# Sums of squares split into two tasks around a chunk of the z projection, with their low part made by VectorE

## The chip, the cores and the metric

The kernel runs on one core of a Trainium2 chip. The metric is the device time of one execution in microseconds (us), lower is better. Five engines work side by side, each through its own queue in a fixed order: TensorE (PE; its weight loads are shown apart as PEld), VectorE (DVE), ScalarE (ACT), GpSimd (POOL) and SyncE (SP), which here issues nearly all DMAs.

## The reference, cut to what matters

A hybrid decoder block on x of 1 x 1024 x 1024 in float32. After an RMS norm, one large projection gives the inputs of two attention branches and of their gates:

```
h = rms_norm(x, g_pre);  proj = h @ w_in
qa, ka, va, fa, za, qb, kb, vb, zb, gates = split(proj)
ya = fox_attention(qa, ka, va, log_sigmoid(fa + b)) * silu(za)      # 8 heads of 64
yb = diff_attention(rope(qb), rope(kb), vb, lam)                    # 4 heads, values of 128
yb = rms_norm(yb, g_subln, 1e-5) * (1 - lam_init) * silu(zb)        # norm over a head's 128 channels
merged = sigmoid(gates_a) * (ya @ w_branch[0]) + sigmoid(gates_b) * (yb @ w_branch[1])
out = x + rms_norm(merged @ w_out, g_post)
```

The change is in the norm inside `yb`: for each of the four diff heads and each of the 1024 positions it needs the sum of 128 squares.

## The kernel before, in words

Float32 products are made from a high and a low part (tiles `hi` and `lo`, or `hT[0]` and `hT[1]`): hi is a rounded copy, lo the difference, and three matmuls stand for one. `project` makes one 128 x 512 chunk of a projection in 24 such matmuls of 512 columns. Its weights come through `load_w`: a DMA into `raw`, hi by GpSimd (line 321), lo by VectorE (line 324).

The work runs in stages: the value projection; eight attention units (u = 0 to 3 diff heads, 4 to 7 pairs of forgetting heads); the gates; the branch products; the output projection. Inside a unit the attention itself is a list of `groups`, each of two score rows (`row`, `s_row`: matmuls into `S`, a VectorE pass with the running minimum, line 495, and an exponential on ScalarE, line 501) and of products (`av`: transposes on TensorE, line 522, hi by ScalarE, line 525, lo by VectorE, line 526, and matmuls into `yp`, line 546). Between the groups stand the `fill` tasks: the four chunks k, q, k, q of the next unit's projection (`unit_proj`), two chunks of one z tile (`z_tasks`, `spill_tasks`: 24 matmuls into `pz`, a copy to SBUF on line 433, a store), and in units 3 to 6 (`SFILL`) the sums of squares of one diff head: `sum_squares` for each half c of the positions and then `subln_scales`.

`sum_squares` loads half of the head's stored output `y_d` (line 442), squares it on ScalarE (443), makes hi on ScalarE (445) and lo on GpSimd (446), adds the 128 channels up by two matmuls with a matrix of ones (`onesr`, lines 448 and 449, into `ssq`), copies the one row out (450) and stores it (451). What it makes is read only after the attention, by `y_work`.

Three rings of buffers bind these steps. `pj` has two PSUM buffers, taken in turn by every k, q and z chunk and by `ssq`. The tag `sw` has two SBUF buffers: hi and lo of the squares take both, and the hi part of a k or q chunk (`stack`, lines 378 and 379, or `rope` for a diff unit) takes one. The tag `raw` has four.

Program order is a priority: a planner puts each engine's instructions into one fixed order by a simulated timeline, and takes what is ready in it, earlier program text first. `tc.issue_after(x)` adds that what is written in its block comes behind x in the order of x's engine. `lasts[0]` holds the last matmul that the program has written so far. How the fill tasks are dealt out is one line in the loop over the groups, where `done` counts the weight (4g + 3) of the groups so far:

```
while nf < len(fill) and nf < len(fill) * done * (3 if u == 7 else 1) / total:
    fill[nf]()
    nf += 1
```

Of the kernel before, what the change touches and what calls it, by code (L numbers as in the profile page):

```python
# [12 lines left out]
ALU = mybir.AluOpType  # L13
# [8 lines left out]
CH = 512  # L22
# [14 lines left out]
ZFILL = ((0,), (1,), (), (2,), (3,), (4,), (5,), (6, 7))  # L37
# [13 lines left out]
def tile_hybrid_block(  # L51
# [18 lines left out]
    nc = tc.nc  # L70
# [28 lines left out]
    onesr = const.tile([P, 32], F32R, name="onesr")  # L99
# [17 lines left out]
    def rstd_of(dst, ss, n, eps):  # L117
        nc.gpsimd.tensor_scalar(dst, ss, 1.0 / n, eps, op0=ALU.mult, op1=ALU.add)
        nc.gpsimd.tensor_tensor(dst, dst, mhalf[:, 0:dst.shape[-1]], op=ALU.pow)
# [220 lines left out]
    with ExitStack() as st:  # L340
# [75 lines left out]
        def z_tasks(t):  # L416
            return spill_tasks(f"z{t}", (ZA + t * P) if t < 4 else (ZB + (t - 4) * P), z_d[t])

        def spill_tasks(nm, c0, dst):
            box = {}  # L420

            def mk(c):
                def run(ks=range(KT)):
                    if not box:
                        box[0] = load_w(nm, w_cols(c0))
                    if ks[0] == 0:
                        box["ps"] = pj.tile([P, CH], F32, tag="pj", name=f"p{nm}_{c}")
                    ps = box["ps"]
                    lasts[0] = project(ps, box[0], c, ks)
                    if ks[-1] < KT - 1:  # L430
                        return
                    zs = stg.tile([P, CH], F32, tag="raw", name=f"s{nm}_{c}", bufs=4)
                    nc.scalar.copy(zs, ps)
                    nc.sync.dma_start(dst[:, c * CH:(c + 1) * CH], zs)
                return run
            return [mk(0), mk(1)]

        def sum_squares(t, c):

            sl = slice(c * CH, (c + 1) * CH)  # L440
            sq = stg.tile([P, CH], F32, tag="raw", name=f"sq{t}_{c}", bufs=4)
            nc.sync.dma_start(sq, y_d[t][:, sl])
            nc.scalar.activation(sq, sq, AF.Square)
            hi, lo = (stg.tile([P, CH], F32R, tag="sw", name=f"sq{part}{t}_{c}") for part in range(2))
            nc.scalar.copy(hi, sq)
            nc.gpsimd.tensor_tensor(lo, sq, hi, op=ALU.subtract)
            ps = pj.tile([P, CH], F32, tag="pj", name=f"ssq{t}_{c}")[0:32]
            nc.tensor.matmul(ps, lhsT=onesr, rhs=hi, start=True, stop=False)
            nc.tensor.matmul(ps, lhsT=onesr, rhs=lo, start=False, stop=True)
            nc.scalar.copy(sq[0:1], ps[0:1])  # L450
            nc.sync.dma_start(ss_d[t:t + 1, sl], sq[0:1])

        def subln_scales(t):
            rs = sub_rs[:, t]
            nc.sync.dma_start(rs, ss_d[t].rearrange("(p j) -> p j", j=8))
            rstd_of(rs, rs, P, SUB_EPS)
            nc.sync.dma_start(rs_d[t].rearrange("(p j) -> p j", j=8), rs)
# [21 lines left out]
        lastx, vload, lasts = [None], [], [None]  # L479
# [74 lines left out]
        def products(trans, prod, g):  # L554
            for jj in range(g + 1 + SKEW):
                if jj <= g:
                    trans(jj)
                if jj >= SKEW:
                    prod(jj - SKEW)
# [91 lines left out]
        def forget_sums():  # L651

            fgf = fg.rearrange("p a b -> p (a b)")
            fs = pp.tile([P, 4, 64], F32, tag="P", name="fs")
            fn, fe, fu, fc = (fs[:, n, :] for n in range(4))
            nc.vector.tensor_scalar(fn, fgf, -1.0, None, op0=ALU.mult)
            nc.vector.tensor_tensor(fn, fn, fgf, op=ALU.min)
            nc.scalar.activation(fe, fn, AF.Exp)
            nc.vector.tensor_scalar(fu, fe, 1.0, None, op0=ALU.add)
            nc.vector.tensor_scalar(fc, fu, -1.0, None, op0=ALU.add)  # L660
            nc.vector.tensor_tensor(fc, fe, fc, op=ALU.subtract)
            nc.scalar.activation(fn, fu, AF.Ln)
            nc.vector.reciprocal(fu, fu)
            nc.vector.tensor_tensor(fc, fc, fu, op=ALU.mult)
            nc.vector.tensor_tensor(fn, fn, fc, op=ALU.add)
            nc.vector.tensor_scalar(fe, fgf, 0.0, None, op0=ALU.min)
            nc.vector.tensor_tensor(fe, fe, fn, op=ALU.subtract)
            lf = pp.tile([8, S], F32, tag="P", name="lf")
            cum = pp.tile([8, S], F32, tag="P", name="cum")
            ones8 = pp.tile([8, S], F32, tag="P", name="ones8")  # L670
            nc.gpsimd.memset(ones8, 1.0)
            for half in range(2):
                tp = tps.tile([P, CH], F32, tag="tp", name=f"ft{half}")
                for q in range(4):
                        b = half * 4 + q
                        nc.tensor.transpose(tp[0:8, q * P:(q + 1) * P], fe[:, b * 8:(b + 1) * 8], ident)
                nc.scalar.copy(lf[:, half * CH:(half + 1) * CH], tp[0:8, :])
            nc.vector.tensor_tensor_scan(cum, ones8, lf, initial=0.0, op0=ALU.mult, op1=ALU.add)
            nc.vector.tensor_scalar(cum, cum, -8.0, None, op0=ALU.mult)
            nc.sync.dma_start(cum_d, cum)  # L680
# [7 lines left out]
        for u in range(8):  # L688
            load, load_v, groups = nxt or unit_attn(u, T)
            nxt = None  # L690
            if u == 0:
                vload.append(load_v)
            if u == 1:
                forget_sums()
            load()
            fill = []
            if u + 1 < 8:
                T, tasks = unit_proj(u + 1)
                fill += tasks
            for t in ZFILL[u]:  # L700
                fill += z_tasks(t)
            for t in SFILL[u]:
                fill += [lambda t=t, c=c: sum_squares(t, c) for c in range(2)]
                fill.append(lambda t=t: subln_scales(t))
            late = [fill.pop(), gate[0]] if u == 7 else []
            total = sum(s[0] for s in groups)
            done, nf = 0, 0
            for n, (wgt, rws, prd) in enumerate(groups):
                if n == len(groups) // 2 and u < 7:
                    nxt = unit_attn(u + 1, T)  # L710
                    vload.append(nxt[1])
                for r in rws:
                    r()
                mark = lasts[0]
                if pend and (u < 7 or n <= TAIL):
                    products(*pend())
                if u == 7 and n >= TAIL:
                    tail.append(prd)
                pend = prd
                done += wgt  # L720
# [3 lines that stand above are left out]
                if u == 7:  # L724
                    for f, a, b in LATE[n]:
                        with tc.issue_after(mark):
                            late[f](range(a, b))
                    if n == GFILL:
                        behind = tuple(held)
                        break  # L730
# [69 lines left out]
    sums = [None]  # L800
# [377 lines left out]
```

## Time and profile before

| what | value |
|---|---|
| median of 3 runs | 900.61 us (899.82 to 900.72) |
| the profiled execution's own time | 901.03 us |
| its span | 899.3 us, so 1.7 us lie around it |
| PE, PEld, DVE, ACT, POOL busy | 98%, 83%, 65%, 48%, 45% of the span |
| granted TensorE clock | 0.998 |

Busy times are shares of the span of one execution. PE counts the matmuls with modelled ends, PEld the weight loads. In an answer by stretches of time, the first number is the length of the stretch and the others are the busy time of each engine in it. In an answer in order of time, a row has its start, its length, its engine and line, what it writes and reads, and in brackets how long the engine was idle before it and what ended that. "PEld ssq L448 <- ACT sq L445: 1.1, 2, 0.8" says that weight loads of `ssq` on line 448 waited twice for ScalarE's line 445, 1.1 us in all and 0.8 us at most.

### The profile page before, as it was taken

How to read it: one execution, taken by the hardware profiler on the slowest of the kernel's cores; microseconds unless marked ns; L12 is line 12 of the kernel's file. 1: busy time of each engine (PE TensorE's matmuls, PEld its weight loads, DVE VectorE, ACT ScalarE, POOL GpSimd, SP SyncE). 2: the span in 40 equal slices, each digit the busy share in tenths (PEclk: the TensorE clock that was granted, in tenths of full speed). 3: DMA queues.
4: the chain of work that ended last, by engine and by line, in shares of the span. 5: the costliest groups of instructions: out<-in, count | busy, mean ns of one | idle time of the engine just before them, and what ended most of it. 6: DMA issues, size and time to landing. Idle time of an engine off the chain costs nothing.

```text
span 899.3 us, 13795 instructions
## 1 busy us (share of the span) xinstructions
PE 882.4 (98%) x4600; PEld 745.4 (83%) x4600; DVE 581.8 (65%) x1122; ACT 430.4 (48%) x865; POOL 406.0 (45%) x398
## 2 busy tenths in 40 slices
PE   8999999999999999999999999999999999999996
PEld 5999987788888878888888888888888888888885
DVE  6766555767666744456647556627766896648896
ACT  7523224665756653364545646724543362314352
POOL 2134224735646535254344435516534323483961
PEclk9999999999999999999999999999999999999999
DMA  8566656756557763645636430397766598210495
GB/s 303 191 241 249 221 160 166 176 139 170 154 136 188 183 172 80 184 98 133 188 94 158 137 105 26 85 410 243 240 200 203 185 359 299 80 39 1 124 194 173
DMA packets 138185, 154.79 MB, mean 172 GB/s; under 512 B 12145, under 2 KB 98161, under 8 KB 137090
## 3 DMA queue, kind: packets, MB, share of 16 engines
q1 hardware_dynamic: 133744, 151.55, 56.2%
q0 software_dynamic: 4224, 2.10, 2.0%
q8 instruction: 36, 0.59, 0.3%
q14 instruction: 35, 0.29, 0.1%
q10 hardware_dynamic: 146, 0.27, 0.1%
HBM read 86.17 MB, written 38.34 MB: 138 GB/s over the span
## 4 chain that ended last, share of the span: by engine, by line
PE 84%; DMA 4%; DVE 3%; ACT 3%; SPq 2%; issue 2%; POOL 2%; POOLq 0%; DVEq 0%; ACTq 0%
PE x_g L818 15%; PE pb L978 10%; PE pv L214 10%; PE pz L334 9%; PE x_o L818 9%; PE pk L334 7%; PE pq L334 6%; PE ypf L546 4%; PE ptf L522 3%; PE ypd L546 2%; PE Sf L492 2%; PE Sf L493 2%; PE pg L334 1%; SPq L366 1%; PE pgl L334 1%
## 5 line engine op out<-in xcount | busy, mean ns | idle before, releaser
L214 PE MATMUL pv<-wvhi,hT 128*128 128x264 f32 (+2 forms) x384 | 88.1, 323 | 1.0 <-ACT wvhi L160 1.0
L334 PE MATMUL pq<-hT,hi_q 128*128 128x512 f32 x256 | 82.1, 395 | 0.0
L334 PE MATMUL pz<-hT,hi_z 128*128 128x512 f32 x256 | 81.7, 394 | 0.3 <-DVE rotq L368 0.2
L334 PE MATMUL pk<-hT,hi_k 128*128 128x512 f32 x256 | 81.7, 393 | 0.0
L978 PE MATMUL pb<-yT,hi_br 128*128 128x512 f32 x256 | 78.8, 389 | 0.0
L818 PE MATMUL x_g<-T,a_g 128*128 128x512 f32 x336 | 78.0, 391 | 0.0
L818 PE MATMUL x_o<-wo_op,a_o 128*128 128x512 f32 x336 | 77.6, 392 | 0.0
L818 PEld LDWEIGHTS x_o<-wo_op,a_o 128*128 128x128 f32 x336 | 63.0, 188 | 14.4 <-DVE a_o L768 0.5
L818 PEld LDWEIGHTS x_g<-T,a_g 128*128 128x128 f32 x336 | 63.1, 188 | 13.8
L214 PEld LDWEIGHTS pv<-wvhi,hT 128*128 128x128 f32 x384 | 64.1, 190 | 7.2 <-ACT wvhi L160 1.7
L526 DVE TENSOR_TENSOR plf<-ptf,phf 128x512 fp32r<-128x512 f32 (+1 forms) x80 | 50.1, 635 | 25.8 <-ACT phf L525 25.1
L501 ACT ACTIVATE Pd<-Pd,mxd 128x128 f32<-128x128 f32 (+7 forms) x64 | 49.8, 778 | 33.6 <-DVE mxd L495 33.5
L618 POOL TENSOR_TENSOR cb<-cb,trim 128x128 f32<-128x128 f32 x64 | 29.3, 462 | 72.0 <-DVE mxf L495 49.9
L214 PE MATMUL pv<-wvlo,hT 128*128 128x256 f32 (+2 forms) x192 | 61.7, 326 | 0.0
L501 ACT ACTIVATE Pf<-Pf,mxf 128x1024 f32<-128x1024 f32 (+3 forms) x64 | 49.7, 777 | 24.4 <-DVE mxf L495 24.1
L818 PE MATMUL x_g<-hT,a_g 128*128 128x512 f32 x252 | 59.1, 392 | 0.0
L623 POOL TENSOR_SCALAR Pf<-Pf,lf 128x1024 f32<-128x1024 f32 (+3 forms) x64 | 47.9, 753 | 21.9 <-DVE lf L622 18.3
L525 ACT CAST phf<-ptf 128x512 fp32r<-128x512 f32 (+1 forms) x80 | 42.6, 543 | 30.7 <-PE ptf L522 26.5
L978 PEld LDWEIGHTS pb<-yT,hi_br 128*128 128x128 f32 x256 | 48.0, 188 | 10.1
L818 PEld LDWEIGHTS x_g<-hT,a_g 128*128 128x128 f32 x252 | 47.3, 188 | 10.4
L334 PEld LDWEIGHTS pz<-hT,hi_z 128*128 128x128 f32 x256 | 47.3, 188 | 9.4 <-DVE rotq L368 0.5
L334 PEld LDWEIGHTS pq<-hT,hi_q 128*128 128x128 f32 x256 | 47.2, 188 | 8.9
(262 smaller groups left out, 2282.1 us busy)
## 6 DMA issues: line engine op xcount, KB each, us to landing
t_d<-t SPq DMA_DIRECT2D x16, 512.0 KB, 4.1
T<-t_d SPq DMA_DIRECT2D x8, 1024.0 KB, 8.3
raw<-in_w_in_dram SPq DMA_DIRECT2D x14, 512.0 KB, 4.8
vb_d<-vbs SPq DMA_DIRECT2D x8, 512.0 KB
va_d<-vas SPq DMA_DIRECT2D x8, 512.0 KB, 3.3
raw_k<-in_w_in_dram SPq DMA_DIRECT2D x8, 512.0 KB, 4.5
raw_q<-in_w_in_dram SPq DMA_DIRECT2D x8, 512.0 KB, 4.7
V<-vb_d SPq DMA_DIRECT2D x4, 1024.0 KB, 6.3
```

Of the source, the lines that this page charges most:

```text
L214: nc.tensor.matmul(ps[n], lhsT=hT[hp][k // 4][i // 4][:, k % 4, hs], rhs=wt[k][:, a:b], start=first, stop=(k == KT - 1 and hp == 1))
L334: mm = nc.tensor.matmul(ps, lhsT=a[:, k, :], rhs=hT[h][k // 4][c][:, k % 4, :], start=(k == 0 and a is hi and h == 0), stop=(k == KT - 1 a ...
L492: nc.tensor.matmul(ps, lhsT=A[:, qs], rhs=B[:, a:b], start=True, stop=False)
L501: held[0] = nc.scalar.activation(pr[:, 0:n], pr[:, 0:n], AF.Exp, bias=mx[:, len(pcs) - 1:len(pcs)], scale=-1.0, accum_out=le).ins
L522: lasts[0] = nc.tensor.transpose(pt[:, o * P:(o + 1) * P], rows[2 * g + r][:, j * P:(j + 1) * P], ident).ins
L525: nc.scalar.copy(ph[:, 0:n], pt[:, 0:n])
L526: nc.vector.tensor_tensor(pl[:, 0:n], pt[:, 0:n], ph[:, 0:n], op=ALU.subtract)
L546: lasts[0] = nc.tensor.matmul(o, lhsT=a, rhs=b[:, src], start=(j == 0 and n == 0), stop=(odd == 1 and jj == g and n == len(prods) - 1)).ins
L618: nc.gpsimd.tensor_tensor(diag, diag, trim, op=ALU.add)
L623: held[1] = nc.gpsimd.tensor_scalar(p1[:, 0:n], p1[:, 0:n], l1, 1.0, op0=ALU.mult, op1=ALU.mult).ins
L818: nc.tensor.matmul(x[m], lhsT=a[:, ai, k, :], rhs=right[m][bi][k], start=(k == 0 and n == 0), stop=(k == 3 and n == 2))
L978: nc.tensor.matmul(ps, lhsT=a[:, kk, :], rhs=yT[g][h][:, k % 2, sl], start=(k == 0 and a is hi and h == 0), stop=(k == 3 and a is lo))
```

## The change

`sum_squares` becomes two tasks. `squares` loads, squares and makes hi and lo; `square_sums` does the two matmuls, the copy and the store. In the list of fill tasks of units 3 to 6 the order was z0, z1, both sums of squares, scales; now it is squares 0, z0, sums 0, squares 1, z1, sums 1, scales. The first matmul of the sums is ordered behind the last matmul written so far, which is the last one of the z chunk. The low part of the squares is made by VectorE in place of GpSimd.

```diff
         def sum_squares(t, c):
 
+            box = {}
+            return lambda: squares(t, c, box), lambda: square_sums(t, c, box)
+
+        def squares(t, c, box):
+
             sl = slice(c * CH, (c + 1) * CH)
             sq = stg.tile([P, CH], F32, tag="raw", name=f"sq{t}_{c}", bufs=4)
             nc.sync.dma_start(sq, y_d[t][:, sl])
             nc.scalar.activation(sq, sq, AF.Square)
             hi, lo = (stg.tile([P, CH], F32R, tag="sw", name=f"sq{part}{t}_{c}") for part in range(2))
             nc.scalar.copy(hi, sq)
-            nc.gpsimd.tensor_tensor(lo, sq, hi, op=ALU.subtract)
+            nc.vector.tensor_tensor(lo, sq, hi, op=ALU.subtract)
+            box.update(sq=sq, hi=hi, lo=lo)
+
+        def square_sums(t, c, box):
+
+            sl = slice(c * CH, (c + 1) * CH)
+            sq, hi, lo = box["sq"], box["hi"], box["lo"]
             ps = pj.tile([P, CH], F32, tag="pj", name=f"ssq{t}_{c}")[0:32]
-            nc.tensor.matmul(ps, lhsT=onesr, rhs=hi, start=True, stop=False)
+            with tc.issue_after(lasts[0]):
+                nc.tensor.matmul(ps, lhsT=onesr, rhs=hi, start=True, stop=False)
             nc.tensor.matmul(ps, lhsT=onesr, rhs=lo, start=False, stop=True)
             nc.scalar.copy(sq[0:1], ps[0:1])
             nc.sync.dma_start(ss_d[t:t + 1, sl], sq[0:1])
...
-            for t in ZFILL[u]:
-                fill += z_tasks(t)
+            z = [f for t in ZFILL[u] for f in z_tasks(t)]
             for t in SFILL[u]:
-                fill += [lambda t=t, c=c: sum_squares(t, c) for c in range(2)]
-                fill.append(lambda t=t: subln_scales(t))
+                z = [f for c in range(2) for sq, sums in [sum_squares(t, c)] for f in (sq, z[c], sums)]
+                z.append(lambda t=t: subln_scales(t))
+            fill += z
```

## The prediction

> **What bounds the kernel now.** I read the page first, then the chain that ended last, then the engines' busy time by stretches of time around the sums of squares, then the rows in order of time at the edges of these stretches, and last the waits of the weight loads.
>
> ```profile
> span 899.3 us, 13795 instructions
> PE 882.4 (98%) x4600; PEld 745.4 (83%) x4600; DVE 581.8 (65%) x1122; ACT 430.4 (48%) x865; POOL 406.0 (45%) x398
> PE 84%; DMA 4%; DVE 3%; ACT 3%; SPq 2%; issue 2%; POOL 2%; POOLq 0%; DVEq 0%; ACTq 0%
> ```
>
> TensorE carries 84% of the chain. So time moves only where TensorE waits, or where it gets more or less to do; this change leaves its instructions as they are. Where does it wait near the sums of squares? The next answer has, in its first four rows, the stretch from the end of the second z chunk of units 3, 4, 5 and 6 to the first matmul of the next projection, and in the other four the stretches ahead of and between them.
>
> ```profile
> core 0: us, PE busy (x) PEld busy (x) DVE busy (x) ACT busy (x) POOL busy (x), PEclk, DMA share, GB/s
> 323.77:332.66 8.89, 8.76 (x50) 6.52 (x48) 7.97 (x20) 6.94 (x14) 2.76 (x3) 1.00 0.62 172
> 379.21:389.34 10.13, 9.15 (x62) 7.69 (x62) 8.12 (x24) 8.69 (x20) 7.07 (x10) 1.00 0.47 119
> 441.03:448.75 7.72, 7.72 (x56) 7.19 (x56) 7.60 (x21) 6.72 (x14) 4.51 (x7) 1.00 0.53 140
> 498.36:507.85 9.49, 8.97 (x59) 7.40 (x59) 7.02 (x18) 7.68 (x16) 4.98 (x6) 1.00 0.51 142
> 291.82:323.77 31.95, 31.95 (x175) 27.64 (x174) 16.25 (x40) 15.77 (x34) 13.78 (x14) 1.00 0.73 184
> 332.66:379.21 46.55, 46.55 (x249) 39.91 (x249) 19.65 (x50) 20.07 (x37) 20.59 (x23) 1.00 0.52 136
> 389.34:441.03 51.69, 51.69 (x293) 44.87 (x292) 27.98 (x76) 24.35 (x54) 19.75 (x31) 1.00 0.53 141
> 448.75:498.36 49.61, 49.61 (x275) 42.89 (x274) 27.81 (x77) 23.96 (x56) 21.52 (x34) 1.00 0.54 143
> ```
>
> In the 179.80 us of the last four rows a projection chunk is always under way, and PE is busy without a gap. In the 36.23 us of the first four there is none: PE has attention alone, DVE is busy for 30.71 us (85%; 51% in the others) and ACT for 30.03 us (83%; 47%), and PE is idle for 36.23 - 34.60 = 1.63 us. So these are short phases in which the softmax engines set the pace, because TensorE has no filler. Why does the next projection not begin at the end of z?
>
> ```profile
> 323.81 0.59 ACT L433 COPY sz<-pz 128x512 f32<-128x512 f32 x1 [4.85 <-PE pz L334]
> 331.95 0.57 ACT L450 COPY sq<-ssq 1x512 f32<-1x512 f32 x1
> 332.57 0.30 PEld L334 LDWEIGHTS pk<-hT,hi_k 128*128 128x128 f32 x2 [0.27 <-ACT sq L450]
> 388.65 0.57 ACT L450 COPY sq<-ssq 1x512 f32<-1x512 f32 x1
> 389.27 0.30 PEld L334 LDWEIGHTS pk<-hT,hi_k 128*128 128x128 f32 x2
> 447.73 0.57 ACT L450 COPY sq<-ssq 1x512 f32<-1x512 f32 x1
> 448.64 0.30 PEld L334 LDWEIGHTS pk<-hT,hi_k 128*128 128x128 f32 x2
> 507.09 0.57 ACT L450 COPY sq<-ssq 1x512 f32<-1x512 f32 x1
> 507.74 0.30 PEld L334 LDWEIGHTS pz<-hT,hi_z 128*128 128x128 f32 x2
> 312.43 1.28 DVE L324 TENSOR_TENSOR lo_k<-raw_k,hi_k 128x1024 fp32r<-128x1024 f32 x1 [0.25 <-POOL hi_k L321]
> ```
>
> In all four units the next chunk's first weight load starts 0.05 to 0.34 us after the end of the first sum's copy (331.95 + 0.57 = 332.52, then 332.57, and so on). Its weights were ready long before (lo_k at 313.71 for the chunk at 332.57). What it waits for is the `pj` buffer: both sums are ahead of it in that ring of two, and they take both buffers after z0 and z1. Their own inputs come late, as lowest priority among the unit's tasks. What TensorE loses meanwhile is seen best at the weight loads, all waits over the whole 216 us:
>
> ```profile
> PEld ssq L448 <- ACT sq L445: 1.1, 2, 0.8
> PEld ypf L546 <- DVE plf L526: 0.8, 2, 0.5
> PEld ptf L522 <- DVE plf L526: 0.6, 1, 0.6
> PEld Sd L492 <- DVE mxd L495: 0.6, 2, 0.3
> PEld ypf L546 <- DVE ys L633: 0.4, 1, 0.4
> PEld ptf L522 <- PE Sf L493: 0.4, 1, 0.4
> PEld ypd L546 <- DVE pld L526: 0.3, 1, 0.3
> PEld ypf L546 <- ACT phf L525: 0.3, 1, 0.3
> PEld pk L334 <- ACT sq L450: 0.3, 1, 0.3
> PEld ssq L449 <- POOL sq L446: 0.2, 1, 0.2
> PEld ypd L546 <- ACT phd L525: 0.2, 1, 0.2
> PEld Sf L492 <- DVE mxf L495: 0.2, 1, 0.2
> ```
>
> They sum to 5.4 us: 1.3 at the sums' own matmuls, 0.3 at the chunk behind them, 3.8 at attention, which mostly waits for DVE or ACT.
>
> **The change, part by part.**
>
> *The order z0, sums 0, z1, sums 1.* In the ring, z1 now follows the first sum, and the next unit's k follows the second. z1 needs the buffer of z0, free when the copy of line 433 is done, and not the end of the squares' chain; the next k needs the buffer of z1 likewise. So the 36.23 us without filler shrink to two short handovers in each unit. By the dealing rule the eleven tasks also fall otherwise than the nine: in unit 3 (weights 3, 7, 11, 15) z1 moves from the third group to the fourth, in units 4 to 6 from the third of eight to the fifth, so filler lasts to later rows. What the stretches lose has three readings: PE idle, 1.63 us; the waits of the weight loads, 5.4 us, of which some lie under matmuls that still run; and density. Weight loads fill 155.31 of 179.80 us = 86.4% where filler exists, but 28.80 of 36.23 us here; at 86.4% the same loads take 33.3 us, 2.9 us less. I take 2.9, the middle one, since it neither counts hidden waits nor the modelled ends; 1.63 and 5.4 stay as ends. The Trainium skill, in Perfetto Trace Analysis, Identifying the Most-Contended Engine, holds that matmul busy time is a bad measure because matmuls overlap, and that the share of weight loads is the better one; by matmul idle time alone the gain would be 1.6 us and the result hard to tell from nothing, by its measure it is 2.9, and the trace bears it out in so far as unfilled stretches show 79% against 86%.
>
> *The handovers.* New are eight places (behind each sum) at which a chunk waits for the copy of the chunk before. z1 of unit 3 ended at 323.77 and its copy at 324.40; with 0.05 us to the next load that is 0.7 us, 5.6 us over eight. If PE has attention ready, it loses in them what it lost in unfilled time, 2.9/36.23 = 8%, so 0.45 us; if nothing, 5.6. Nothing is no lower end, since the two matmuls of the sum fill part of each. I take 0.5: PE was still 95% busy (34.60 of 36.23) without filler.
>
> *The order behind the z chunk.* A row of the chain gives the pace of z:
>
> ```profile
> 315.99 7.79 PE pz L334 x34
> ```
>
> At 7.79/34 = 0.23 us a chunk of 24 takes at least 5.5 us, and hi and lo are now written ahead of one. So the 1.3 us of waits at lines 448 and 449 go; they are inside the 2.9 already. Next late would be `sw`: the second squares need both buffers back from the first sum's matmuls, and have the whole of z1 for it. Ahead of the first squares stands the next unit's last q chunk, whose hi holds one; z0 covers that.
>
> *lo on VectorE.* The trace has the same operation with its source in PSUM and in SBUF, and the one that leaves GpSimd:
>
> ```profile
> L379 DVE TENSOR_TENSOR lok<-pk,hik x8: 670/683/692, 285.6 to 472.1; 128x512 fp32r<-128x512 f32 x8
> L379 DVE TENSOR_TENSOR lok<-rotk,hik x6: 689/846/2051, 148.3 to 274.9; 128x512 fp32r<-128x512 f32 x6
> L446 POOL TENSOR_TENSOR sq<-sq,sq x8: 1285/1301/1306, 329.2 to 506.9; 128x512 fp32r<-128x512 f32 x8
> ```
>
> The squares lie in SBUF, so the nearest row is `rotk`: 8 x 0.85 = 6.8 us more on VectorE (5.5 to 16.4 by that row's shortest and longest), 10.4 us less on GpSimd. Its cover is that VectorE is 51% busy while filler runs, and the squares now lie there. I cost it at nothing; without cover it costs up to its 6.8.
>
> *Moved with it.* Per unit ScalarE's two squares and two hi casts leave the unfilled phase for the filled one, where it is 47% busy; SyncE issues the two loads of `y_d` and the first store earlier, in the same number, past z1's store; GpSimd's queue loses four-fifths of this task. Nothing reads the sums before the attention ends, so their own time is free: zero.
>
> *The last unit.* The fourth stretch gives 9.49 - 7.40/0.864 = 0.9 us of the 2.9. What it brings forward is unit 7's own filler, and behind it PE will run out of filler the sooner. I count half: 0.45 back.
>
> *Sum.* -2.9 + 0.5 + 0.45 = -1.95, about -2.0 us. On the profiled execution that is 901.03 - 2.0 = 899.0; it lies 0.4 above the median of the runs, so on the median 900.61 - 2.0 = **898.6 us**. A change of 0.2%, 1.8 us, is about what can be told from none here.
>
> **The rivals.** *The stream stays blocked.* The next unit's k could still wait, for the rows that read the same `KA` and `TA` buffers (two each), or because the planner uses the freed time elsewhere. Then only the 1.3 us at the sums' matmuls go: 899.3 us, no difference. For it: the next unit's q weights are made by GpSimd only when z1 is done. Against: k's weights are ready 19 us early and every chunk starts right at the copy.
>
> *The handovers bite* (slower). The planner counts on the copy of `pz` earlier than ScalarE does it, and PE, whose order is fixed, stands with nothing behind it: 8 x 0.7 = 5.6 us less the 2.9 gained is +2.7, 903.3 us. It decides from 0.36 us lost on average at each. For it: ScalarE is the busiest helper in these phases, 83%. Against: where k, q and z chunks follow each other now, no PE wait of that kind is in the list above.
>
> *VectorE is held up* (slower). GpSimd waited for hi 11.9 us in five of eight cases (the view of line 446, what its engine sat idle for):
>
> ```profile
>   ACT sq L445: 11.9, 5
> ```
>
> If VectorE's fixed order inherits such waits next to line 495 or 526, attention behind it waits too; with a quarter of them exposed, 11.9/4 = 3.0 us against 2.0, 901.6. The page SBUF — State Buffer of the Trainium skill, Who interferes with whom, says that a VectorE operation with two SBUF inputs and a GpSimd one that reads SBUF block each other for the whole instruction. The row of `rotk` against `pk` (846 against 683 ns, up to 2051) agrees. Against: a two-input GpSimd operation of 1.3 us goes away in exchange.
>
> **How the numbers follow.** The filler closes the stretches: 0.62, between 895.6 (5.4 less 0.45) and 900.0 (1.63 less both givebacks of 0.95); of it 0.47 beyond 1.8 us and 0.15 within. Blocked as before: 0.14, within. Handovers: 0.15, slower. VectorE: 0.09, of it 0.07 slower, 0.02 within. That makes faster 0.47, same 0.31, slower 0.22. The range goes from the lower end, 895.6, to the handovers' 903.3; since half the rest lies on the other side, the likeliest case's own range is 895.6 to 900.0.
>
> **What the changed profile would show.** Right: between the end of each z chunk and the next projection chunk 1 to 2 us instead of 8 to 10; no wait at the matmuls of `ssq`; PE busy throughout from 292 us to the end of unit 6, and unit 7 beginning 2 us earlier; GpSimd's busy time 10 us down, VectorE's 5 to 9 up. Wrong: new waits of `pz` or `pk` for line 433; lines 495 or 526 late behind the new VectorE operation; or the same gain lost again in the waits of unit 7, after 510 us, where filler runs out.

## The result, and the profile after

The changed kernel takes 905.35 us in the median of six runs (902.98 to 907.90), the kernel before on the same chip 900.24 (898.46 to 900.79): a ratio of 1.0053, 95% interval 1.0038 to 1.0067. It is slower by 0.5%. The forecast was 898.6 us, with a range of 895.6 to 903.3; the time lies outside it, on the other side. The profiled execution took 906.38 us. Some executions of `b_vector`, `p_vector`, `a_free` and `p_copy` took 1773 us or more; the medians below leave them out, and the profile of `p_vector` is of such a one.

The first lines of the page of the changed kernel:

```profile
span 904.6 us, 13826 instructions
PE 884.3 (98%) x4600; PEld 745.7 (82%) x4600; DVE 584.1 (65%) x1130; ACT 430.9 (48%) x865; POOL 398.0 (44%) x390
```

GpSimd lost 8 us, VectorE gained 2.3, and there are 4600 matmuls as before. The next answer, by stretches of time, has first the ends of the second z chunk of units 3 to 6 up to the next projection chunk (the four stretches of 8 to 10 us of before), then two stretches that matter below: the one ahead of unit 6's z, and the one in unit 7. The second fence has the kernel before in the same two places. The third has the four places between z0 and z1 in the changed kernel, which in the kernel before had no gap.

```profile
core 0: us, PE busy (x) PEld busy (x) DVE busy (x) ACT busy (x) POOL busy (x), PEclk, DMA share, GB/s
328.79:332.06 3.27, 2.51 (x15) 1.79 (x13) 2.73 (x7) 2.83 (x7) 3.19 (x3) 1.00 0.19 43
386.92:389.19 2.27, 2.27 (x17) 2.08 (x16) 2.24 (x4) 1.73 (x4) 0.15 (x1) 1.00 0.39 138
442.40:444.27 1.87, 1.87 (x16) 1.63 (x14) 0.83 (x1) 1.78 (x4) 1.00 (x1) 1.00 0.38 117
499.37:502.19 2.82, 2.63 (x19) 2.15 (x18) 2.76 (x10) 1.53 (x4) 0.93 (x2) 1.00 0.93 320
475.17:480.88 5.71, 3.83 (x28) 3.33 (x27) 4.05 (x10) 3.89 (x11) 2.38 (x4) 1.00 0.71 164
527.25:543.06 15.81, 14.98 (x101) 12.04 (x101) 13.51 (x42) 12.21 (x30) 6.13 (x13) 1.00 0.29 90
```

```profile
473.90:480.20 6.30, 6.30 (x37) 5.49 (x36) 4.21 (x12) 2.47 (x5) 2.98 (x4) 1.00 0.76 183
530.45:539.56 9.11, 8.77 (x59) 7.29 (x58) 8.08 (x24) 6.84 (x16) 2.64 (x6) 1.00 0.31 93
```

```profile
318.79:321.90 3.11, 2.50 (x11) 1.33 (x10) 2.95 (x7) 1.74 (x5) 0.68 (x1) 1.00 0.88 226
375.35:377.71 2.36, 2.36 (x18) 2.18 (x17) 2.21 (x5) 2.20 (x5) 0.00 (x0) 1.00 0.17 65
430.30:433.00 2.70, 2.70 (x20) 2.03 (x19) 2.63 (x10) 2.67 (x7) 1.45 (x2) 1.00 0.36 78
489.39:491.22 1.83, 1.83 (x11) 1.07 (x10) 1.74 (x6) 1.78 (x6) 0.00 (x0) 1.00 0.82 205
```

So the stream is unblocked, as forecast: behind z1 36.2 us without filler became 10.2. With the 10.0 us between z0 and z1 it is 20.2, in eight places of 1.8 to 3.3 us where 1 to 2 were forecast. But ahead of unit 6's z a stretch of 5.71 us has appeared in which TensorE stands still for 1.9, where it was busy throughout; and unit 7's stretch has grown from 9.1 to 15.8 us.

To compare kernels with different orders I count, from each trace, the matmuls issued, each weighed by its width (0.2265 us at 512 columns, about the usual spacing there, 0.171 at 384, 0.114 at 256, 0.0575 at 128), and note how long TensorE took from one amount of this work to the next. The columns are the kernel before, the changed one, a second profile of the same order (the run without the ordering, below), and two experiments:

| time in the kernel before | what lies there | before | changed | again | `p_a_even` | `p_a_all` |
|---|---|---|---|---|---|---|
| 307.7 to 362.1 | unit 3's z and sums | 54.4 | 56.1 | 56.7 | 56.3 | 54.8 |
| to 473.7 | units 4, 5, half of 6 | 111.6 | 109.2 | 109.4 | 109.2 | 109.3 |
| to 500.9 | unit 6's z | 27.2 | 30.5 | 29.9 | 29.9 | 30.5 |
| to 560.4 | unit 7 | 59.5 | 60.3 | 60.4 | 58.4 | 58.5 |
| to 692.4 | end of attention, gates | 132.0 | 132.0 | 131.9 | 132.0 | 132.0 |
| to 742.8 | gates, branch products | 50.4 | 52.3 | 50.5 | 52.7 | 52.5 |

The 5.3 us between the two profiles are +1.7, -2.4, +3.3, +0.8, 0.0 and +1.9. Of these the last is in one profile of the changed order and not in the other. A row is good to some 0.3 us, since it depends on the weights. The border at 500.9 us is less sharp: counted without the matmuls of the sums, which lie in other places in the two kernels, unit 6's z takes 4.3 us more and unit 7 nothing. The waits of the weight loads over the same chunks (291.82 to 502.19 us), of which before had many small ones, none longer than 0.8 us, begin so in the changed kernel:

```profile
PEld ypf L558 <- DVE plf L538: 2.1, 1, 2.1
PEld pk L334 <- ACT sz L433: 1.2, 1, 1.2
PEld ssq L461 <- DVE sq L451: 1.0, 1, 1.0
```

Lines behind 460 are 12 higher than before: 558 is 546, 538 is 526, 507 is 495. The second and the third wait are unit 3's. In order of time:

```profile
318.30 1.73 DVE L451 TENSOR_TENSOR sq<-sq,sq 128x512 fp32r<-128x512 f32 x1 [2.01 <-ACT sq L450]
320.08 0.42 PE L461 MATMUL ssq<-sq,onesr 128*32 128x512 f32 x1 [0.59 <-DVE sq L451]
330.51 1.03 ACT L606 ACTIVATE Pd<-Pd,l 128x896 f32<-128x896 f32 x1
331.44 0.56 ACT L433 COPY sz<-pz 128x512 f32<-128x512 f32 x1
332.06 0.73 PE L334 MATMUL pk<-hT,hi_k 128*128 128x512 f32 x2 [0.76 <-ACT sz L433]
```

The chunk z1 ended at 328.8; its copy stood behind two softmax steps on ScalarE until 331.44, and the next k waited for it. The first wait is the end of a chain through four queues:

```profile
469.84 0.39 SPq L314 DMA_DIRECT2D raw_z<-in_w_in_dram  x1
471.65 0.33 SPq L590 DMA_DIRECT2D cb<-cum_d  x1
474.77 0.40 PE L334 MATMUL pq<-hT,lo_q 128*128 128x512 f32 x1
476.16 0.46 POOL L630 TENSOR_TENSOR cb<-cb,trim 128x128 f32<-128x128 f32 x1 [2.98 <-DMA cb<-cum_d]
476.59 1.05 POOL L321 TENSOR_SCALAR hi_z<-raw_z 128x1024 fp32r<-128x1024 f32 x1
477.68 1.47 DVE L324 TENSOR_TENSOR lo_z<-raw_z,hi_z 128x1024 fp32r<-128x1024 f32 x1 [1.16 <-POOL hi_z L321]
479.07 0.55 DVE L538 TENSOR_TENSOR plf<-ptf,phf 128x384 fp32r<-128x384 f32 x1
479.67 0.38 PE L558 MATMUL ypf<-plf,V 128*128 128x256 f32 x1 [1.88 <-DVE plf L538]
479.82 0.66 DVE L379 TENSOR_TENSOR lok<-pk,hik 128x512 fp32r<-128x512 f32 x1
480.88 0.62 PE L334 MATMUL pz<-hT,hi_z 128*128 128x512 f32 x2
```

The load of `cb` lands by 476.16; GpSimd, which trims it, makes `hi_z` only then, VectorE's `lo_z` follows, and behind that stand attention's low part and `lok`, which frees the buffer for z. TensorE's last projection matmul was at 474.77. The kernel before has the same late load, at the same time:

```profile
476.21 0.88 POOL L618 TENSOR_TENSOR cb<-cb,trim 128x128 f32<-128x128 f32 x2 [3.93 <-DMA cb<-cum_d]
479.20 1.06 POOL L321 TENSOR_SCALAR hi_z<-raw_z 128x1024 fp32r<-128x1024 f32 x1
481.41 0.39 PE L334 MATMUL pq<-hT,lo_q 128*128 128x512 f32 x1
```

There the q chunk lasts until 481.41 and covers it. In the changed kernel the filler ran ahead of the attention and was used up 6.6 us earlier, while the load did not come earlier.

### The profile page after: what moved, and what is told of

It reads as the page before. It is cut to its first block, busy times and chain, and to the rows that moved or that the text cites. A ratio compares the mean times of both kernels' runs of the same rounds, so it can differ in the third digit from the quotient of the medians.

```text
span 904.6 us, 13826 instructions
## 1 busy us (share of the span) xinstructions
PE 884.3 (98%) x4600; PEld 745.7 (82%) x4600; DVE 584.1 (65%) x1130; ACT 430.9 (48%) x865; POOL 398.0 (44%) x390
## 5 line engine op out<-in xcount | busy, mean ns | idle before, releaser
L630 POOL TENSOR_TENSOR cb<-cb,trim 128x128 f32<-128x128 f32 x64 | 31.4, 491 | 87.3 <-DVE mxf L507 61.0
L635 POOL TENSOR_SCALAR Pf<-Pf,lf 128x1024 f32<-128x1024 f32 (+3 forms) x64 | 48.0, 753 | 30.5 <-DVE lf L634 28.3
L507 DVE CUSTOM_DVE_ANT_0 Pf<-Sf,cb 128x512 f32<-128x512 f32 (+1 forms) x64 | 36.2, 568 | 30.6 <-PE ptf L534 21.0
L604 POOL TENSOR_SCALAR Pd<-Pd,l,nlam 128x128 f32<-128x128 f32 (+7 forms) x32 | 30.2, 942 | 58.5 <-DVE l L603 54.5
```

The source lines that it names most:

```text
L507: nc.vector.tensor_tensor_reduce(out=pr[:, a:b], in0=ps, in1=bias[:, boff + a:boff + b], scale=-0.125, scalar=BIG if j == 0 else mx[:, j - ...
L604: nc.gpsimd.tensor_scalar(p2[:, 0:n], p2[:, 0:n], l2, nlam, op0=ALU.mult, op1=ALU.mult)
L630: nc.gpsimd.tensor_tensor(diag, diag, trim, op=ALU.add)
L635: held[1] = nc.gpsimd.tensor_scalar(p1[:, 0:n], p1[:, 0:n], l1, 1.0, op0=ALU.mult, op1=ALU.mult).ins
```

## The experiments

Each time stands beside the kernel before on the same chip (medians 899.49 to 900.88). In the expectations from `b_none` on, theory A is that filler is a fixed amount, so that what covers units 3 to 6 is missing later, and rival B that the single new waits and VectorE's operation make the loss. Most edits of the text make the planner lay out a new order; a name that begins with p has its orders pinned.

**One part alone.** `a_pool`: the change with lo left on GpSimd.

```diff
-            nc.vector.tensor_tensor(lo, sq, hi, op=ALU.subtract)
+            nc.gpsimd.tensor_tensor(lo, sq, hi, op=ALU.subtract)
```

> The changed kernel with the squares' low part back on GpSimd. If VectorE's new operation is what costs (rival 'VectorE is held up'): back to within 1.5 us of before, 899 to 902. If the new order of tasks is what costs (sums between the z chunks, eleven tasks dealt instead of nine): stays at 903 to 907. If both share it: about 902.5.

904.98 us, 1.0053 (1.0034 to 1.0072): as the changed kernel. So taking the operation off VectorE gains nothing that can be measured, in an order close to the changed one (204 of 4600 matmuls stand elsewhere). `b_vector` is the opposite edit in the kernel before.

> Before with VectorE's low part alone. VectorE theory: 903 or more. Order theory: 898.5 to 902, no difference that can be told, with VectorE's busy time about 5.5 to 7 us up and GpSimd's 10 us down. In the stretches without filler VectorE is already 85% busy, so a loss would show there as waits of weight loads above 5.4 us.

908.86 us, 1.0096 (1.0074 to 1.0118). But here the planner also found another order. `p_vector` is the same edit with every engine's order pinned to that of before.

> Before with VectorE's low part alone, as in b_vector, but with every engine's order pinned to the plan of before: only the eight operations change their engine. Theory of the plan (any edit makes the planner lay out hundreds of instructions anew, and the new orders wait more than the old one): 898 to 901, against b_vector's 909. VectorE theory (the operation itself holds attention up): 905 or more, as in b_vector.

903.37 us, 1.0031 (1.0017 to 1.0046), between what the two theories gave. So in the old order the eight operations do cost, some 2.8 us; where is open, as no profile of this version can be compared. The rest of `b_vector`'s loss, about 6 us by the two ratios, comes from its new order. `a_free` is the change without the ordering behind the z chunk.

```diff
-            with tc.issue_after(lasts[0]):
-                nc.tensor.matmul(ps, lhsT=onesr, rhs=hi, start=True, stop=False)
+            nc.tensor.matmul(ps, lhsT=onesr, rhs=hi, start=True, stop=False)
```

> The changed kernel without the ordering behind the z chunk. The planner's order is the same instruction for instruction on all five engines, so this part of the change does nothing and the run is a second profile of the changed kernel: 903 to 907. What its profile shares with the first (waits near 320, 332 and 480 us) belongs to the order; what it doesn't share is scatter between executions.

907.05 us, 1.0056 (1.0035 to 1.0076). All five engines have the same order as in the changed kernel: this part does nothing. Its profile is the column "again".

**The dealing and the ring.** `b_dealt` is the kernel before with its sums whole behind z1, but dealt as eleven tasks by empty ones.

```diff
-                fill += [lambda t=t, c=c: sum_squares(t, c) for c in range(2)]
+                none = lambda: None
+                z = [none, z[0], none, none, z[1], both, lambda t=t: subln_scales(t)]
```

> Before with the dealing of the changed kernel alone: empty tasks are put into the list so that z0 and z1 fall to the same groups as in the changed kernel, both sums of squares stay whole and behind z1, and GpSimd makes the low part. If the later place of z1 among the groups is what costs: 903 or more. If the split and the handovers between sums and chunks cost: 899 to 902.

908.30 us, 1.0086 (1.0066 to 1.0106). `a_nine` is the change dealt as nine: squares 0, z0, sums 0 and squares 1 are one task.

> The changed kernel's instructions and program order, dealt to the groups as nine tasks instead of eleven (squares 0, z0, sums 0 and squares 1 as one task, z1, sums 1, an empty one, the scales). If the later dealing of z1 and of the sums (eleven tasks) costs by itself, as the kernel before lost 8 us with that dealing, this comes back to 900 to 902 us. Theory A has the early filler as the cause, which dealing as nine makes earlier if anything: 904 to 908 us, with unit 7's longest stretch at 14 us or more. Rival B: 904 to 907 us, with stretches that do not matter.

903.50 us, 1.0035 (1.0022 to 1.0047): a little better than the change at most, since the intervals overlap, and between the forecasts. So the later dealing, with the order that the planner makes of it, costs 8 us in the old text; how much of the change's loss it makes, these two don't settle. The trace of `a_nine` says something else: its stretches behind z1 are almost as long as before (5.3, 7.8, 9.4 and 10.3 us, 33.0 in all against 36.2), the longest between unit 7's z chunks is 3.4 us, and it loses 2.8 us all the same. So filler that ran ahead is not what every loss here comes from. `b_ring` unblocks the stream in another way: the kernel before, with the sums in the ring of the transposes.

```diff
-            ps = pj.tile([P, CH], F32, tag="pj", name=f"ssq{t}_{c}")[0:32]
+            ps = tps.tile([P, CH], F32, tag="tp", name=f"ssq{t}_{c}")[0:32]
```

> Before with the sums' PSUM tile taken from the transposes' ring of two buffers in place of the projections' ring. It unblocks the next projection and changes no task, no engine and no dealing. My prediction's main term says the blocked stretches cost 2.9 us: 897.3 to 898.6, and the stretches from the last z to the next projection shrink from 8 to 10 us to 1 to 2. If filler there is worth nothing, because it is only missing later: 900 to 901.5, with the waits moved behind 510 us. If the transposes now wait for the sums' buffer: over 902.

904.91 us, 1.0054 (1.0034 to 1.0074). Nothing of the sums stands between z1 and the next k here, there is no new operation on VectorE, and the loss in time is the same. By the count of the table it lies elsewhere in part: 2.9 us from 362.1 to 473.7 us and 2.8 in unit 7, whose long stretch is here too (16.4 us), and none in unit 6's z. That the transposes wait for the sums' buffer is not the reason; their weight loads waited 0.4 us for it in all.

**Is any new order worse?** An order that has been tuned might lose by whatever moves it. `n_copy` is an edit that has nothing to do with this: the sum's copy on VectorE. The planner moved 325 of TensorE's 4601 instructions. (By the order of the matmuls in the traces, 387 of 4600 stand elsewhere than before here, and 626 in the changed kernel.) `p_copy` is the same with the order pinned.

```diff
-            nc.scalar.copy(sq[0:1], ps[0:1])
+            nc.vector.tensor_copy(sq[0:1], ps[0:1])
```

> An edit that has nothing to do with the change: in before, the copy of the one row of sums (line 450, 0.57 us, eight times) is made by VectorE in place of ScalarE. The plan moves 325 of 4601 TensorE instructions. Theory of the plan: 902 to 909. If new plans are not worse as such: 898.5 to 901.5, since 8 x 0.6 us on engines that are not the bound is nothing.

> The same unrelated edit, with the order of all engines pinned to the plan of before. Theory of the plan: 898 to 901. If the copy on VectorE itself costs: the same as n_copy.

900.65 us, 0.9995 (0.9986 to 1.0004), and 900.76, 0.9998 (0.9989 to 1.0007). So a new order need not cost anything. It can: `b_vector`'s cost about 6 us. That part of the loss is only an order less lucky than the old one is therefore not excluded by these runs; the moves of single instructions below test it piece by piece.

**No sums at all.** `b_none` is the kernel before without them; it leaves out their loads, squares, matmuls, copies and stores, and the scales are worked out from a constant.

> The kernel before without any sums of squares (their loads, squares, matmuls, copies and stores are left out, 16 of 13795's small matmul instructions among them; the scales are worked out from a constant instead). It has less work on every engine, and nothing stands between z and the next projection in the ring. Theory A: the filler runs ahead as in the changed kernel, so in spite of less work the time is not lower than before by more than the 16 matmuls' 4 us: 899 to 904 us (ratio 0.998 to 1.004), with the longest stretch of unit 7 at 13 to 17 us. Rival B (handovers and VectorE): without sums nothing waits, so the work that is left out and the 2.9 us of the stretches are gained: 894 to 897 us.

903.62 us, 1.0033 (1.0020 to 1.0045). The time fell where theory A put it, in part for another reason. Without sums the four scales depend on nothing, and were made at the start, ahead of the first norm:

```profile
2.96 6.50 POOL L119 TENSOR_TENSOR sub_rs<-sub_rs,mhalf 128x8 f32<-128x8 f32 x4
```

At the first row of the table this kernel is at 313.4 us instead of 307.7, so 5.7 us are lost there, and the time says little. Its trace says more: the two holes are there without any operation of the change. Counted without the matmuls of the sums, unit 6's z takes 2.5 us more than before, and unit 7 0.6 less.

```profile
473.30:480.60 7.30, 5.87 (x43) 4.88 (x41) 4.23 (x12) 3.55 (x10) 3.79 (x5) 1.00 0.59 162
525.60:540.45 14.85, 13.94 (x98) 11.71 (x98) 11.71 (x36) 10.63 (x27) 5.26 (x12) 1.00 0.29 97
```

**Holding the filler back.** `a_hold` and `r_hold`: in units 4 to 7 the first fill task comes behind the last score row of the first group, in the changed kernel and in `b_ring`.

```diff
-                    fill[nf]()
+                    with tc.issue_after(mark) if u >= 4 and n == nf == 0 else ExitStack():
+                        fill[nf]()
```

> The changed kernel, with one thing added: in units 4 to 7 the first fill task is ordered behind the last score row of the unit's first group, so that the next unit's projection cannot begin earlier than that. Theory A (filler is a fixed amount: in the changed kernel it runs ahead of the attention, and what the stretches without filler gain in units 3 to 6 is lost again in unit 7 and in one stall near 475 to 481 us): holding it back brings the time down, to 899.5 to 903 us (ratio 0.999 to 1.003), and the longest stretch without a projection chunk in unit 7, 16.0 us in the changed kernel, becomes 9 to 11 us as it was before. Rival B (the loss lies in the single handovers and in VectorE's operation, wherever the filler stands): 904 to 907 us, as the changed kernel. Rival C (TensorE cannot be without filler at the start of a unit): worse, above 907 us.

> The kernel before with the sums' PSUM tile taken from another ring (that alone measured 904.9 us) and the same order as in the other kernel of this call: in units 4 to 7 the first fill task behind the last score row of the first group. Theory A: near the kernel before, 899 to 902.5 us, and the longest stretch of unit 7, 16.5 us without the order, 9 to 11 us. Rival B has no handover behind a sum and no VectorE operation here, so it has no account of the 904.9 and expects no change, 904 to 906 us. Rival C: above 907 us.

908.38 us, 1.0079 (1.0065 to 1.0093), and 917.88, 1.0195 (1.0181 to 1.0210). Both missed, and came out as rival C had it: TensorE lacks filler at the start of a unit. Unit 7's long stretch went, but each unit got one at its start, in `a_hold` of 13.2, 13.3 and 14.6 us, the first of them:

```profile
387.30:400.50 13.20, 12.47 (x87) 10.55 (x86) 11.34 (x35) 10.27 (x27) 7.56 (x14) 1.00 0.58 166
```

Filler held back in whole chunks is missing in one piece. The test was too coarse to decide on theory A.

**Moving single instructions.** From here every engine's order is pinned to the changed kernel's own, and only the named instructions move. `p_a_even` spreads 19 matmuls of unit 7's chunk z7a, in six parts, over the long stretch; `p_b_even` does so with 13 in the kernel before.

> The changed kernel with every engine's order pinned to its own plan, except that 19 matmuls of unit 7's chunk z7a are taken out of the place behind 519 us and spread in six parts over the stretch 527 to 543 us, where the changed kernel has no projection chunk (its copy and store follow it). Theory A (what is gained in units 3 to 6 is lost in unit 7, whose filler ran ahead): the stretch of 16.0 us goes, of the 5.7 us lost in it 2 to 3.2 come back: 902 to 903.5 us (ratio 1.002 to 1.0035, from 1.0053). Rival B (the single waits near 320, 332 and 480 us make the loss): no change, 904.5 to 906 us. Rival D (attention loses the same whether filler stands in it or not): no change either, with the loss shown in the short gaps between the parts instead.

> The kernel before with every engine's order pinned to its own plan, except that 13 matmuls of unit 7's chunk z7a are spread in four parts over its stretch 530.4 to 539.6 us. The stretch lost 2.5 us in 9.3, so by theory A there is less to gain than in the changed kernel: 0.5 to 1.5 us, 899 to 900 us (ratio 0.9983 to 0.9995). Rival D: 1.000. A ratio above 1.001 would say that spreading filler costs as such.

904.16 us, 1.0046 (1.0028 to 1.0064), and 900.38, 1.0003 (0.9992 to 1.0015). The same stretch of time in `p_a_even`:

```profile
527.25:543.06 15.81, 15.81 (x99) 14.03 (x99) 12.96 (x44) 11.01 (x26) 6.87 (x13) 1.00 0.27 80
```

TensorE has no idle time in it, and unit 7 takes 58.4 us instead of 60.3: 1.9 less in the trace. The median is 1.2 lower, which the intervals don't separate; it lies between theory A's range and the rivals'. For the kernel before there was nothing to gain, where theory A had 0.5 to 1.5 us.

`p_a_waits` was to move the three waits: the copy of unit 3's z1 up, the second matmul of the first sum down, and on VectorE `lo_z` behind attention's low part.

> The changed kernel with every engine's order pinned to its own plan, except for three single moves: VectorE's lo of the weights z5 behind one low part of attention's products (ahead of it TensorE waited 2.0 us at 479.7), ScalarE's copy of z2's second half ahead of two softmax steps (0.9 us at 332.1), and the second matmul of the first sum behind two score matmuls (0.8 us at 320.1). Rival B: the three waits go, 3 to 3.7 us, so 901.7 to 902.5 us. Theory A: they are a smaller part, up to the 2.0 of the one that before had not at all: 903.3 to 904.8 us. Rival D: the waits appear a few us later elsewhere, 904.5 to 906.

908.14 us, 1.0094 (1.0074 to 1.0115). The edit took the `lo_z` of z5 instead of z6's, and so became a test of the chain:

```profile
472.07 0.39 SPq L314 DMA_DIRECT2D raw_z<-in_w_in_dram  x1
472.56 0.53 SPq L590 DMA_DIRECT2D cb<-cum_d  x1
478.57 0.45 POOL L630 TENSOR_TENSOR cb<-cb,trim 128x128 f32<-128x128 f32 x1 [5.04 <-DMA cb<-cum_d]
480.07 1.47 DVE L324 TENSOR_TENSOR lo_z<-raw_z,hi_z 128x1024 fp32r<-128x1024 f32 x1 [4.05 <-POOL hi_z L321]
482.06 0.58 PE L558 MATMUL ypf<-plf,V 128*128 128x256 f32 x1 [4.78 <-DVE plf L538]
```

z5's lo was later, so the load of `raw_z` into its buffer was (472.07 against 469.84). `cb`, queued behind it, went out 0.9 us later and took 6.0 us to its use instead of 4.5, 2.4 us in all, and TensorE's wait grew from 1.88 to 4.78 us. So a delay of one operation on VectorE goes through the four queues to TensorE: the chain is shown by that. What breaking it would gain is not. In unit 3 the two other moves together gained nothing: that row of the table takes 56.0 us, against 56.1. `p_a_both` has the edits of `p_a_waits` and `p_a_even`.

> Both edits together: unit 7's chunk spread and the three waits moved. If A and B are both parts of it, the gains add: 899.5 to 901.5 us, the time of the kernel before, with neither the stretch nor the three waits in the trace. If it is rival D, 904 to 906 us.

907.82 us, 1.0090 (1.0067 to 1.0113): the longer wait is in it too. `p_a_cb` moves one load on SyncE's queue (the lines are the queue's order, not program text).

```diff
-raw_z7<-w_in
 cb6_1<-cum_d
+raw_z7<-w_in
```

> The changed kernel, every engine's order pinned to its own plan, with one move on SyncE's queue: the load of raw_z7 (512 KB, needed only after 499 us) goes behind the load of cb6_1 instead of ahead of it. Chain theory: TensorE's wait of 2.0 us at 479.7 is the end of a chain (lo_z5 on VectorE frees a weight buffer, raw_z7's load takes it, cb6_1's load is queued behind and lands 4.5 us after its issue, GpSimd's trim of cb waits for it, hi_z6 behind that on GpSimd, lo_z6 on VectorE, the low part of attention's products behind that). Then cb lands about 1.5 to 3 us earlier and the wait shrinks to 0 to 0.6 us: 903 to 904.3 us (ratio 1.003 to 1.0045). If the wait comes from VectorE's own order alone, it stays at 2 us: 905 to 906.

906.41 us, 1.0068 (1.0049 to 1.0087). Missed:

```profile
470.09 0.33 SPq L590 DMA_DIRECT2D cb<-cum_d  x1
474.23 0.46 POOL L630 TENSOR_TENSOR cb<-cb,trim 128x128 f32<-128x128 f32 x1 [2.61 <-DMA cb<-cum_d]
477.74 0.39 PE L558 MATMUL ypf<-plf,V 128*128 128x256 f32 x1 [1.51 <-DVE plf L538]
```

From issue to use `cb` took 4.1 us instead of 4.5, and the wait shrank by 0.37. So the place behind `raw_z` was not the main thing. In the changed kernel too `cb` went out only 1.4 us after SyncE was done with `raw_z` (471.65, against 469.84 + 0.39). What it waited for stands in the waits of SyncE's queue:

```profile
SPq L590 <- DVE lf L634: 1.4, 1, 1.4
```

In `p_a_cb` it is the same line, 4.9 us. Line 634 follows the score pass that reads a tile `cb` on VectorE, so the load most likely waited for its buffer; that was not tested.

`p_a_all` has `p_a_cb`'s move, `p_a_even`'s, the copy of unit 3's z1 up, and attention's low part ahead of the right `lo_z`.

> The changed kernel pinned as before, with the move of cb6_1, the low part of attention's products ahead of lo_z6 on VectorE, the copy of z2's second half ahead of two softmax steps, and unit 7's chunk spread over 527 to 543 us. If the loss is the sum of the stall near 480 us (2.9 more than before in that stretch), unit 7 (0.9) and the handover (0.9), 905.35 - 2.9 - 1.2 - 0.5 gives about 900.8 us: 900 to 902.5 us, the time of the kernel before or a little above. If what is taken away comes back elsewhere, 903.5 to 905.5 us.

902.90 us, 1.0024 (1.0011 to 1.0036), better than the changed kernel and not as good as the one before; no version is faster than that. Units 3 and 7 are mended (54.8 and 58.5 us in the table). Unit 6 is not; there the one wait has become two:

```profile
477.42 0.50 PE L504 MATMUL Sf<-KA,TA 128*128 128x512 f32 x1 [0.67 <-DVE mxf L507]
478.93 0.69 PE L334 MATMUL pz<-hT,hi_z 128*128 128x512 f32 x2 [0.78 <-DVE lok L379]
```

Both are for VectorE, behind the same `lo_z`: with the low part out of its way, the score pass and `lok` come late next. To take `lo_z` behind all of them was not tried, so no run has taken back the 3.3 us of unit 6's z.

## Why the prediction was wrong

*The stretches, -2.9.* Right in kind: from 362.1 to 473.7 us, with the z chunks of units 4 and 5, the changed kernel needs 2.4 us less (2.2 in the second profile). In size it is luck that this is near 2.9. For the two stretches that lie there the share of weight loads gives 10.13 - 7.69/0.864 = 1.2 and 7.72 - 7.19/0.864 = -0.6, 0.6 us together; unit 3, to which the same measure gives a gain of 8.89 - 6.52/0.864 = 1.3, lost 1.7. So it was no measure of a single stretch, nor of the kernel: the step took it that a filled stretch stays won. The filler is the same 24 matmuls a chunk, so it only moved forward, and left what it had covered. (The rival that the stream stays blocked fell with it: 36.2 us became 20.2.)

*The last unit, +0.45.* Right in kind; the size lies between 0 and 0.8, as one counts. Unit 7's stretch grew by 6.7 us and the unit by 0.8 at most; `p_a_even` takes back 1.9, more than the change had added.

*No term at all: unit 6's z, +3.3 (2.7 in the second profile).* This is the step that failed, and the largest part of the loss. The text asked of each stretch what would cover it, and of unit 7 what would be uncovered; it did not ask the same of the stretches between, whose rows say that PE is busy without a gap. That was true because filler lay over a load that lands at 476.2 us. What the runs showed in its place is a stretch of 5.71 us without filler, in which TensorE stands still for 1.9, at the end of the chain from `cb`; that the whole 3.3 us come from it is argued, since no run removed it. A list of the helpers that are late while filler runs (GpSimd idle 3.93 us for `cb`, in the row of before) would have shown what is exposed if filler ends 6 us sooner. In kind it is the rival "VectorE is held up", which stood at 0.09 and 901.6 us: a wait on VectorE with attention behind it, though at line 324 and not at the new operation.

*The handovers, +0.5.* In the eight places TensorE stands still for 1.6 us in all, by the rows above. Of the waits for a chunk's copy the trace shows one, 0.76 us at unit 3's k; with the wait of 0.59 at the first sum unit 3 costs 1.7 us more (2.3 in the second profile). "No wait at the matmuls of `ssq`" was wrong there: hi and lo were not ready ahead. In units 4 to 6 there is none of either kind. `p_a_all` brings unit 3 back to 0.4.

*lo on VectorE, 0.* Right within the change (`a_pool`). Outside it, in the old order, wrong: 2.8 us. VectorE's busy time rose by 2.3 us, not by 5 to 9. The row of `rotk`, 846 ns and up to 2051, was the right neighbour; in the changed kernel:

```profile
L451 DVE TENSOR_TENSOR sq<-sq,sq x8: 681/893/1726, 318.3 to 497.5; 128x512 fp32r<-128x512 f32 x8
```

*The ordering, inside the 2.9.* It has no effect on any engine's order (`a_free`).

*The sum.* By work done: +1.7 - 2.4 + 3.3 + 0.8 = +3.4 us where -2.0 was forecast. The medians differ by 5.1. The rest is open: 0.1 to 1.9 us lie behind 692 us, partly in a wait for line 980 that one profile of the changed order has and the other has not,

```profile
PE pb L990 <- DVE yT L980: 1.0, 2, 0.8
```

and what makes it appear was not found: `n_copy`, as fast as the kernel before, loses 1.8 us there too. By the same count all five pinned versions of the changed order lose 1.2 to 2.2 us there, and `p_b_even` and `p_copy`, with the old order, at most 0.2; so it goes with the order, though `a_free` escaped it. In `p_a_all` it is the size of what is left to the kernel before.

## What to carry to other kernels

Filler that covers waits is a fixed amount. Before unblocking it in one place, list what is late under it everywhere behind (idle times of the helper engines that TensorE does not feel), because it may run out there, and price those waits; here 2.4 us were gained and 3.3 lost in one such place. And an edit of the program's text is an edit of every engine's order: the same eight operations cost 0.96% in a new order and 0.31% in the pinned one. Pin the order, move one instruction, and a cause can be tested within a microsecond or two.

## What the runs showed of the hardware

A long wait of TensorE cost more than its length. In `p_a_waits` TensorE stands still from 477.28 to 482.06 us:

```profile
475.85:479.26 3.41, 1.44 (x10) 1.10 (x8) 0.17 (x1) 1.03 (x5) 0.69 (x2) 1.00 1.02 265
479.26:482.06 2.80, 0.00 (x0) 0.00 (x0) 1.99 (x3) 1.07 (x3) 1.20 (x2) 0.50 0.48 109
482.06:486.08 4.02, 4.02 (x13) 3.44 (x14) 3.96 (x13) 1.34 (x4) 0.85 (x2) 0.50 0.49 106
```

The granted clock fell to 0.50 at 479.26, 2.0 us after the last matmul, and stayed there for 4.0 us of work behind the wait; by that clock, as an estimate, 2 us are lost on top. The Trainium skill, in TensorE: Matmul & The Clock Gate, Part 1: The HAM clock gate, says that the clock is halved after an idle window of about 3.4 us; the trace agrees that it is halved, and differs on the window, since in the 3.41 us ahead of the fall TensorE was busy for 1.44. In `r_hold` it fell at 525.12 us, inside a gap of 1.44 us, with TensorE busy for 1.49 us of the 3.41 ahead:

```profile
521.71:525.12 3.41, 1.49 (x11) 1.14 (x10) 1.43 (x6) 3.34 (x10) 3.41 (x6) 1.00 0.37 85
525.12:531.95 6.83, 6.35 (x25) 5.57 (x26) 3.14 (x10) 3.36 (x10) 3.03 (x6) 0.50 0.06 12
```

So a stretch that is only thin was enough. In the changed kernel's profile the clock stayed at 1.00 through the wait at 479.67 us.
